# A written order for three engines, from the output projection to the FFN's activation sums of a decoder layer

## The chip, the cores and the metric

The kernel runs on one core of a Trainium2 chip. The metric is the device time of one execution in microseconds (us); lower is better. Engines: TensorE (PE) multiplies matrices and transposes, VectorE (DVE), ScalarE (ACT) and GpSimd (POOL) work elementwise, SyncE (SP) issues the DMAs. Each engine runs its own queue in order; semaphores make one wait for another.

## The reference

One decoder layer on a sequence of 1024 tokens of width 1024, in float32. What matters here is the second half of the mixer and the start of the FFN (D_FF is 2816):

```python
m = jnp.concatenate([rmsnorm(a, attn_group_norm[i]),
                     rmsnorm(c, conv_group_norm[i])], axis=-1)
x = x + rmsnorm(m @ w_out[i], mix_post_norm[i])
h = rmsnorm(x, ffn_pre_norm[i])
f = (jax.nn.silu(h @ w_gate[i]) * (h @ w_up[i])) @ w_down[i]
```

Here `a` is the causal attention's output, `c` the gated convolution's; `rmsnorm` divides a row by its root mean square and multiplies by a gain.

## The kernel before

**Numbers.** Every float32 operand of a matmul is split into a high part (a cast to the type float32r, on ScalarE) and a low part (the operand minus the high part, on VectorE or GpSimd); `split` issues the cast and the subtraction one behind the other. A product is three matmuls: high by high, high by low, low by high.

**Memory.** `mr` and `mf` are arenas of 2 KB units in on-chip memory for split and for plain float32 data. They hand out the units that were freed longest ago within a named region; `ML` is the region of 22 units (eleven row tiles) in which rows of y, x and the raw copies live. `ps` hands out the eight banks of the accumulator memory in turn.

**Output projection.** Tokens are eight tiles of 128 rows (T = 8). The convolution's half of the projection has been done before and waits in memory as y. For tile t, `wo_a` multiplies the attention half (24 matmuls with 512 columns, into two banks), adds y on VectorE (L1071) and issues the mean square of the sum on ScalarE (L230); `rstd_of` makes the reciprocal root of it, an addition on VectorE (L226) and a power on GpSimd (L227). `wo_x1` applies the norm and its gain (L1077), adds the rows of x (L1079), stores x1 and issues the second mean square. `wo_n` applies the FFN's norm (L1086), in place. `h2_turn` transposes the tile with eight PE transposes (L1106) into two banks, one for each half of the width (q = 0, 1), and makes of them a plain copy (L1108, L1110) and a split for the FFN's right operands. The loop runs over T + 3 steps with the tiles staggered: step t does `wo_a(t)`, `wo_x1(t-1)`, `wo_n(t-2)` and `h2_turn(t-3)`.

**FFN.** The gate and up products are done in 2 by 2 blocks with seven products in place of eight. B11 and B21 are the two halves of the width for tokens 0 to 511, B12 and B22 for tokens 512 to 1023. Three products use blocks as they are (B11, B21, B22); four use the activation sums T3 = B22 - B12, T2 = T3 + B11, T1 = B22 - T2 and T4 = B21 - T2, each 2048 columns wide on VectorE, split by `t_split`. Raw B11 and B21 go through memory (`hr_d`). Weights come in pairs `fp` of two 128-column blocks for gate and up (m = 0, 1); `raw_load` fetches them, `factor` makes the left operand of product p (sums on VectorE for pair 0, on GpSimd otherwise) and splits it, `product` does twelve matmuls and takes the bank's result out. The products 1 and 2 of pairs 0, 1 and 2 need no activation sum and are done first; then a loop over all that is left follows, five factors ahead.

**Order.** The program is written as one stream, and a scheduler decides the order of each engine's queue from it by its own model of times.

Of the kernel before, what the change touches and what calls it, by code (L numbers as in the profile page):

```python
# [135 lines left out]
def hybrid_layer(ctx: ExitStack, tc: tile.TileContext, x, x_t, p_t, cols_in, positions,  # L136
# [924 lines left out]
    def row_norm(t, i):  # L1061
        r = ss_y[:, 2 * t + i : 2 * t + i + 1]
        junk = mr(2, BJ)
        mean_sq(junk.a, rows_y[t].a, D, r)
        free(junk)
        rstd_of(r)

    def wo_a(t):
# [2 lines left out]
        dve.scalar_tensor_tensor(y, b, ss_a[:, t : t + 1], y, op0=ALU.mult, op1=ALU.add)  # L1071
        ps.put(ids)
        row_norm(t, 0)

    def wo_x1(t):
# [5 lines left out]
        sp.dma_start(x1_d[t * P : (t + 1) * P, :], y)
        row_norm(t, 1)

    def wo_n(t):
        y = rows_y[t].a
        dve.scalar_tensor_tensor(y, y, ss_y[:, 2 * t + 1 : 2 * t + 2], g_ffn.a, op0=ALU.mult,  # L1086
                                 op1=ALU.mult)

# [7 lines left out]
    def h2_turn(t):  # L1096
        src = rows_y.pop(t)
# [4 lines left out]
        for q in range(2):  # L1102
            ids, b = ps.get()
            for j in range(4):
                k = 4 * q + j
                pe.transpose(b[:, j * P : (j + 1) * P], src.a[:, k * P : (k + 1) * P], ident[:])  # L1106
# [146 lines left out]
    head = [(0, m, p) for p in (1, 2) for m in range(2)]  # L1253
    for t in range(T + 3):
        if t < T:
            wo_a(t)
        elif t == T:
            for d in (mTa, wo):
                for h, l in d.values():
                    free(h, l)  # L1260
            for i in head[:2]:
                product(*i)
        elif t == T + 1:
            for i in head[2:]:
                product(*i)
# [352 lines left out]
```

## Time and profile before

| | |
|---|---|
| median of 3 runs | 1230.39 us (1228.6, 1230.39, 1286.19) |
| the profiled execution | 1227.49 us |
| its span, first to last instruction | 1225.4 us |
| mean granted TensorE clock | 0.990 |
| busy in the span: PE, DVE, ACT, POOL | 1201.5, 810.6, 587.3, 503.8 us |

The profile shows one execution. A row of the timeline has the start, the duration, the engine, the line in the code, the operation with output and input, and in brackets the idle time before it and what ended it. Where a row shows x2, two instructions that follow each other were merged. A row of the stages has the stretch, its length, each engine's busy time, the granted clock as a share of full speed, the DMA engines' busy share and GB/s.

### The profile page before, as it was taken

How to read it: one execution, taken by the hardware profiler on the slowest of the kernel's cores; microseconds unless marked ns; L12 is line 12 of the kernel's file. 1: busy time of each engine (PE TensorE's matmuls, PEld its weight loads, DVE VectorE, ACT ScalarE, POOL GpSimd, SP SyncE). 2: the span in 40 equal slices, each digit the busy share in tenths (PEclk: the TensorE clock that was granted, in tenths of full speed). 3: DMA queues.
4: the chain of work that ended last, by engine and by line, in shares of the span. 5: the costliest groups of instructions: out<-in, count | busy, mean ns of one | idle time of the engine just before them, and what ended most of it. 6: DMA issues, size and time to landing. Idle time of an engine off the chain costs nothing.

```text
span 1225.4 us, 16706 instructions
## 1 busy us (share of the span) xinstructions
PE 1201.5 (98%) x5918; PEld 1012.2 (83%) x5918; DVE 810.6 (66%) x1173; ACT 587.3 (48%) x1079; POOL 503.8 (41%) x392
## 2 busy tenths in 40 slices
PE   8999999999999999789999999999999999999998
PEld 6998888889999888678788888888888888888886
DVE  6676346478867758785657665565556677758775
ACT  7543333267766736543433333333345546545652
POOL 4433534226554311025888646674634102202321
PEclk8999999999999999889999999999999999999999
DMA  8712553994561667524465445543566576654342
GB/s 267 258 39 104 184 202 133 278 365 90 135 161 44 232 223 252 203 104 143 161 229 197 140 144 190 178 157 118 209 209 200 184 242 230 233 172 164 120 136 79
DMA packets 89821, 217.77 MB, mean 178 GB/s; under 512 B 9030, under 2 KB 18026, under 8 KB 88426
## 3 DMA queue, kind: packets, MB, share of 16 engines
q1 hardware_dynamic: 89392, 216.17, 53.4%
q8 instruction: 46, 0.75, 0.3%
q10 hardware_dynamic: 346, 0.54, 0.2%
q14 instruction: 37, 0.30, 0.1%
HBM read 145.38 MB, written 71.04 MB: 177 GB/s over the span
## 4 chain that ended last, share of the span: by engine, by line
PE 80%; DVE 6%; DMA 5%; issue 3%; ACT 3%; POOL 2%; ACTq 0%; POOLq 0%; DVEq 0%; SPq 0%
PE banks L1192 10%; PE banks L1195 10%; PE banks L1194 10%; PE banks L220 7%; PE banks L222 7%; PE banks L221 7%; PE banks L1391 6%; PE banks L1390 6%; PE banks L1389 6%; PE banks L894 2%; DVE mem_r L210 2%; PE banks L1498 1%; PE banks L1501 1%; PE banks L1500 1%; PE banks L865 1%
## 5 line engine op out<-in xcount | busy, mean ns | idle before, releaser
L210 DVE TENSOR_TENSOR mem_r<-mem_f,mem_r 128x512 fp32r<-128x512 f32 (+1 forms) x404 | 374.4, 958 | 206.4 <-ACT mem_r L209 194.1
L209 ACT CAST mem_r<-mem_f 128x512 fp32r<-128x512 f32 (+2 forms) x407 | 258.4, 666 | 410.6 <-PE banks L1194 128.7
L1192 PE MATMUL banks<-mem_r 128*128 128x512 f32 x616 | 242.0, 393 | 4.5 <-ACT mem_r L209 3.4
L1194 PE MATMUL banks<-mem_r 128*128 128x512 f32 x616 | 241.6, 392 | 0.0
L1195 PE MATMUL banks<-mem_r 128*128 128x512 f32 x616 | 240.8, 392 | 0.1
L220 PE MATMUL banks<-mem_r 128*128 128x512 f32 (+2 forms) x536 | 196.3, 371 | 2.4 <-ACT mem_r L209 1.7
L221 PE MATMUL banks<-mem_r 128*128 128x512 f32 (+2 forms) x536 | 196.4, 368 | 1.3 <-POOL mem_r L210 1.2
L222 PE MATMUL banks<-mem_r 128*128 128x512 f32 (+2 forms) x536 | 196.0, 368 | 0.0
L1192 PEld LDWEIGHTS banks<-mem_r 128*128 128x128 f32 x616 | 116.5, 189 | 30.7 <-ACT mem_r L209 5.0
L1195 PEld LDWEIGHTS banks<-mem_r 128*128 128x128 f32 x616 | 116.7, 189 | 25.7 <-DVE mem_r L210 1.1
L1194 PEld LDWEIGHTS banks<-mem_r 128*128 128x128 f32 x616 | 116.8, 190 | 24.3 <-DVE mem_r L210 0.2
L1391 PE MATMUL banks<-mem_r 128*128 128x512 f32 x308 | 119.8, 389 | 0.0
L1390 PE MATMUL banks<-mem_r 128*128 128x512 f32 x308 | 119.8, 389 | 0.0
L1389 PE MATMUL banks<-mem_r 128*128 128x512 f32 x308 | 119.8, 390 | 0.0
L220 PEld LDWEIGHTS banks<-mem_r 128*128 128x128 f32 x536 | 101.2, 190 | 19.1 <-ACT mem_r L209 2.8
L221 PEld LDWEIGHTS banks<-mem_r 128*128 128x128 f32 x536 | 101.6, 190 | 17.4 <-POOL mem_r L210 1.4
L222 PEld LDWEIGHTS banks<-mem_r 128*128 128x128 f32 x536 | 101.5, 189 | 16.1
L879 POOL TENSOR_TENSOR mem_f<-mem_f,stats 128x640 f32<-128x640 f32 (+5 forms) x64 | 73.4, 1161 | 92.0 <-DVE stats L878 49.4
L227 POOL TENSOR_TENSOR small<-small,mhalf 128x1 f32<-128x1 f32 (+2 forms) x46 | 37.6, 821 | 177.5 <-DVE small L226 177.0
L1210 DVE TENSOR_TENSOR mem_f<-banks,mem_f 128x512 f32<-128x512 f32 x66 | 45.2, 686 | 55.9 <-PE banks L1195 55.8
L210 DVE TENSOR_TENSOR mem_r<-banks,mem_r 128x512 fp32r<-128x512 f32 (+3 forms) x118 | 69.3, 612 | 12.9 <-ACT mem_r L209 12.3
L1390 PEld LDWEIGHTS banks<-mem_r 128*128 128x128 f32 x308 | 57.8, 188 | 12.0
(197 smaller groups left out, 1890.0 us busy)
## 6 DMA issues: line engine op xcount, KB each, us to landing
sc_d<-mem_f SPq DMA_DIRECT2D x77, 256.0 KB, 3.5
mem_f<-sc_d SPq DMA_DIRECT2D x77, 256.0 KB, 3.0
mem_f<-in_w_gate_dram SPq DMA_DIRECT2D x22, 512.0 KB, 5.2
mem_f<-in_w_up_dram SPq DMA_DIRECT2D x22, 512.0 KB, 5.1
mem_f<-in_w_down_dram SPq DMA_DIRECT2D x22, 512.0 KB, 4.5
wc_d<-mem_f SPq DMA_DIRECT2D x22, 512.0 KB, 2.7
mem_f<-wc_d SPq DMA_DIRECT2D x44, 256.0 KB, 3.1
mem_f<-in_w_down_dram SPq DMA_DIRECT2D x33, 256.0 KB, 3.4
```

What stands on the lines that cost most here:

```text
L209: act.copy(h, src)
L210: (eng or dve).tensor_tensor(l, src, h.bitcast(F32), op=ALU.subtract)
L220: pe.matmul(o, wh, vh, start=i == 0, stop=False)
L221: pe.matmul(o, wh, vl, start=False, stop=False)
L222: pe.matmul(o, wl, vh, start=False, stop=i == n - 1)
L879: pool.tensor_tensor(pt.a[:, 0:n], pt.a[:, 0:n], sm.to_broadcast([P, n]), op=ALU.mult)
L1192: pe.matmul(b, wh.a[:, c], th[:, k], start=first and k == 0, stop=False, skip_group_check=True)
L1194: pe.matmul(b, wh.a[:, c], tl[:, k], start=False, stop=False, skip_group_check=True)
L1195: pe.matmul(b, wl.a[:, c], th[:, k], start=False, stop=k == 3, skip_group_check=True)
L1389: pe.matmul(b, ah.a[:, c], bh.a, start=first, stop=False, skip_group_check=True)
L1390: pe.matmul(b, ah.a[:, c], bl.a, start=False, stop=False, skip_group_check=True)
L1391: pe.matmul(b, al.a[:, c], bh.a, start=False, stop=last, skip_group_check=True)
```

## The change

The stretch from the loop to the last activation sum is put under a manual schedule for PE, DVE and ACT: these three queues take the instructions of the stretch in the order in which the code writes them (later instructions may still be put between them); POOL and SP are scheduled as before. For this the helpers are cut in pieces. `row_norm` becomes `row_sq` and `row_rstd`; `h2_turn` becomes `turn_pe` (transposes), `turn_cast`, `turn_copy`, `turn_dve` (subtractions) and `turn_put`; `factor` becomes `factor_a` (sums and cast) and `factor_d` (subtraction); `product` becomes `product_mm` and `product_end`; `t_split` becomes `t_cast` and `t_low`. `wo_n` writes the norm into the rows that held x, not in place. T2, and later T4, are made in B12's buffer instead of one of their own. Pair 2's first half is loaded into the row region `ML`. y of a tile is loaded one step ahead instead of two.

```diff
     def wo_x1(t):
...
-        free(xr)
+        rows_n[t] = xr
         sp.dma_start(x1_d[t * P : (t + 1) * P, :], y)
-        row_norm(t, 1)
+        row_sq(t, 1)
     def wo_n(t):
-        y = rows_y[t].a
-        dve.scalar_tensor_tensor(y, y, ss_y[:, 2 * t + 1 : 2 * t + 2], g_ffn.a, op0=ALU.mult,
+        y = rows_y.pop(t)
+        dve.scalar_tensor_tensor(rows_n[t].a, y.a, ss_y[:, 2 * t + 1 : 2 * t + 2], g_ffn.a, op0=ALU.mult,
                                  op1=ALU.mult)
+        free(y)
...
+    def turn_cast(t):
+        for q, b, h, l in turn_places(t):
+            act.copy(h, bank3(b, 4))
+
+    def turn_copy(t):
...
+        for q, (ids, b) in enumerate(turned[t]):
             if first:
                 act.copy(raw.a[:, q * U : (q + 1) * U], b)
             else:
                 act.copy(four(tr[q])[:, :, o], bank3(b, 4))
...
+    def turn_dve(t, only):
+        for q, b, h, l in turn_places(t):
+            if q == only:
+                dve.tensor_tensor(l, bank3(b, 4), h.bitcast(F32), op=ALU.subtract)
...
+    def wo_step(t, fill=()):
         if t < T:
+            wo_mm(t)
+        for i in fill:
+            factor_a(*i)
+        if t >= 3:
+            turn_cast(t - 3)
+        if 1 <= t <= T:
+            wo_a(t - 1)
+        if t >= 3:
+            turn_copy(t - 3)
+        if 2 <= t <= T + 1:
+            row_rstd(t - 2, 1)
+        for i in fill:
+            factor_d(*i)
+        if t >= 3:
+            turn_dve(t - 3, 0 if t - 3 < T // 2 else 1)
+        if 2 <= t <= T + 1:
+            wo_n(t - 2)
+        if 1 <= t <= T:
+            row_rstd(t - 1, 0)
+        if t >= 3:
+            if t - 3 < T // 2:
+                turn_dve(t - 3, 1)
+            turn_put(t - 3)
+        if 2 <= t <= T + 1:
+            turn_pe(t - 2)
         if 1 <= t <= T:
             wo_x1(t - 1)
         if t < T:
             load_x(t)
...
+        if 1 <= t < T - 1:
+            load_y(t + 1)
+    EN = mybir.EngineType
+    with tc.manual_schedule(engines={EN.PE, EN.DVE, EN.Activation}):
+        for t in range(T):
+            wo_step(t, {1: ((0, 0, 1), (0, 1, 1)), 2: ((0, 0, 2), (0, 1, 2))}.get(t, ()))
...
+        both(product_mm, 0, 1)
+        wo_step(T)
...
+        both(product_mm, 0, 2)
+        wo_step(T + 1)
...
+        raw_load(2, 0, ((0, 22),))
...
+        both(factor_a, 1, 1)
+        product_end(0, 0, 2)
+        factor_d(1, 0, 1)
+        product_mm(1, 0, 1)
...
+        t_sum(b12.a, b22.a, b12.a, ALU.subtract)
+        both(product_mm, 1, 2)
+        t_cast("T3", b12.a)
+        both(product_end, 1, 1)
+        factor_a(0, 0, 6)
+        t_low("T3", b12.a)
+        factor_d(0, 0, 6)
+        factor_a(2, 0, 1)
+        t_sum(b12.a, b12.a, b11, ALU.add)
+        factor_d(2, 0, 1)
+        product_end(1, 0, 2)
+        product_mm(2, 0, 1)
...
+        t_sum(b12.a, b21, b12.a, ALU.subtract)
+        both(factor_a, 0, 5)
+        both(factor_d, 0, 5)
```

VectorE's queue within the loop, before, about a step and a half of it (L226 the addition of `rstd_of`, L1077 and L1079 `wo_x1`, L210 from banks the subtraction of `h2_turn`, L1071 `wo_a`, L1086 `wo_n`):

```order
L226 TENSOR_SCALAR small<-small 128x1
L1077 SCALAR_TENSOR_TENSOR mem_f<-mem_f,small 128x1024
L226 TENSOR_SCALAR small<-small 128x1
L1079 TENSOR_TENSOR mem_f<-mem_f 128x1024
L210 TENSOR_TENSOR mem_r<-banks,mem_r 128x4x128
L1071 SCALAR_TENSOR_TENSOR mem_f<-banks,small,mem_f 128x1024
L210 TENSOR_TENSOR mem_r<-banks,mem_r 128x4x128
L1086 SCALAR_TENSOR_TENSOR mem_f<-mem_f,small 128x1024
```

VectorE's queue for one step now (L1077 `wo_a`, L1145 `turn_dve`, L1094 `wo_n`, L1083 and L1085 `wo_x1`); every step from the third to the sixth reads so:

```order
L1077 SCALAR_TENSOR_TENSOR mem_f<-banks,small,mem_f 128x1024
L226 TENSOR_SCALAR small<-small 128x1
L1145 TENSOR_TENSOR mem_r<-banks,mem_r 128x4x128
L1094 SCALAR_TENSOR_TENSOR mem_f<-mem_f,small 128x1024
L226 TENSOR_SCALAR small<-small 128x1
L1145 TENSOR_TENSOR mem_r<-banks,mem_r 128x4x128
L1083 SCALAR_TENSOR_TENSOR mem_f<-mem_f,small 128x1024
L1085 TENSOR_TENSOR mem_f<-mem_f 128x1024
```

The tile's norm `wo_n` now stands in each step between the two subtractions of the tile ahead of it, and `wo_x1` of the next tile behind both.

ScalarE's queue at the first transposed tile, before (L230 the mean squares, L1108 the copy of a bank, L209 its cast):

```order
L230 ACTIVATE mem_r,small<-mem_f 128x1024 x7
L1108 COPY mem_f<-banks 128x512
L209 CAST mem_r<-banks 128x4x128
L1108 COPY mem_f<-banks 128x512
L209 CAST mem_r<-banks 128x4x128
L230 ACTIVATE mem_r,small<-mem_f 128x1024
```

And now (L1219 the cast of `factor_a`, L1126 of `turn_cast`, L1135 the copy of `turn_copy`):

```order
L230 ACTIVATE mem_r,small<-mem_f 128x1024 x2
L1219 CAST mem_r<-mem_f 128x512 x2
L230 ACTIVATE mem_r,small<-mem_f 128x1024 x2
L1126 CAST mem_r<-banks 128x4x128 x2
L230 ACTIVATE mem_r,small<-mem_f 128x1024
L1135 COPY mem_f<-banks 128x512 x2
```

Before, copy and cast of a bank followed each other; now both casts come first, then the mean square of `wo_a`, then both copies.

VectorE's queue around the first activation sums, before (L1303 a sum, L210 2048 wide the subtraction of `t_split`, L210 512 wide that of `factor`):

```order
L1303 TENSOR_TENSOR mem_f<-mem_f 128x2048
L210 TENSOR_TENSOR mem_r<-banks,mem_r 128x4x128
L1303 TENSOR_TENSOR mem_f<-mem_f,mem_r 128x2048
L210 TENSOR_TENSOR mem_r<-mem_f,mem_r 128x2048
L210 TENSOR_TENSOR mem_r<-mem_f,mem_r 128x512
L1303 TENSOR_TENSOR mem_f<-mem_f 128x2048
```

And now (L1308 a sum, L1317 `t_low`, L1189 `factor_d`, L1205, L1206 and L1214 sums of pair 0's factors, L1260 the addition of `product_end`):

```order
L1308 TENSOR_TENSOR mem_f<-mem_f 128x2048
L1205 TENSOR_TENSOR mem_f<-mem_f 128x512
L1206 TENSOR_TENSOR mem_f<-mem_f 128x512
L1214 TENSOR_TENSOR mem_f<-mem_f 128x512
L1317 TENSOR_TENSOR mem_r<-mem_f,mem_r 128x2048
L1189 TENSOR_TENSOR mem_r<-mem_f,mem_r 128x512
L1308 TENSOR_TENSOR mem_f<-mem_f,mem_r 128x2048
L1189 TENSOR_TENSOR mem_r<-mem_f,mem_r 128x512
L1260 TENSOR_TENSOR mem_f<-banks,mem_f 128x512
```

Sums of pair 0's factors now stand between the first activation sum and its subtraction, and the subtraction for pair 2's first factor, the last L1189, behind T2's sum.

More of the change, by code (lines that the diff above doesn't have):

```diff
@@ L1094, in four, with turn_pe, turn_places @@
         return b.a.rearrange("p (k c) -> p k c", k=4)
-    def h2_turn(t):
-        src = rows_y.pop(t)
+    turned = {}
+    def turn_pe(t):
+        src = rows_n.pop(t)
+        turned[t] = [ps.get(), ps.get()]
+        for q, (ids, b) in enumerate(turned[t]):
+            for j in range(4):
+                k = 4 * q + j
+                pe.transpose(b[:, j * P : (j + 1) * P], src.a[:, k * P : (k + 1) * P], ident[:])
+        free(src)
+    def turn_places(t):
+        o = slice(t % 4 * P, (t % 4 + 1) * P)
+        for q, (ids, b) in enumerate(turned[t]):
+            if t < T // 2 or q:
+                h, l = tf["B" + "12"[q] + "12"[t >= T // 2]]
+                yield q, b, four(h)[:, :, o], four(l)[:, :, o]
+    def turn_cast(t):
+        for q, b, h, l in turn_places(t):
+            act.copy(h, bank3(b, 4))
+    def turn_copy(t):
         o = slice(t % 4 * P, (t % 4 + 1) * P)
@@ L1101, in h2_turn @@
             raw = mf(2, ML)
[L1102 to L1106, printed above, removed]
+        for q, (ids, b) in enumerate(turned[t]):
             if first:
@@ L1188, in product @@
         th, tl = (four(v) for v in tf[RIGHT[p]])
-        first, last = p in (1, 2, 5), p in (2, 3, 4)
+        first = p in (1, 2, 5)
         for k in range(4):
@@ L1252, in hybrid_layer, with both, t_sum, t_cast @@
     tr[0], tr[1] = mf(4, ((22, 26),)), mf(4, ((26, 30),))
-    head = [(0, m, p) for p in (1, 2) for m in range(2)]
-    for t in range(T + 3):
-        if t < T:
[L1256 to L1265, printed above, removed]
+    def both(f, fp, p):
+        for m in range(2):
+            f(fp, m, p)
+    def t_sum(o, x, y, op):
+        dve.tensor_tensor(o, x, y, op=op)
+    def t_cast(n, v):
+        if n not in tf:
+            tf[n] = pair(4, BT)
+        act.copy(tf[n][0].a, v)
+    def t_low(n, v):
+        h, l = tf[n]
+        dve.tensor_tensor(l.a, v, h.a.bitcast(F32), op=ALU.subtract)
+    def wo_step(t, fill=()):
+        if t < T:
+            wo_mm(t)
[23 more added lines that the diff above has]
+            turn_pe(t - 2)
         if 1 <= t <= T:
@@ L1281, in hybrid_layer @@
-        if t + 2 < T:
-            load_y(t + 2)
-        if t == T - 1:
-            raw_load(0, 1, ML)
-        if t == T:
-            raw_load(1, 0, ML)
-        if t == T // 2:
-            for i in head:
-                factor(*i)
-    b12, b22 = tr[0], tr[1]
-    def both(f, fp, p):
-        for m in range(2):
-            f(fp, m, p)
-    def t_split(n, v):
-        if n not in tf:
-            tf[n] = pair(4, BT)
-        h, l = tf[n]
-        split(h.a, l.a, v)
-    def t_sum(o, x, y, op):
-        dve.tensor_tensor(o, x, y, op=op)
```

124 lines of the change are left out of this document (75 added, 49 removed).

## The prediction

> **What bounds the kernel now.** I read the shares and the slices on the page first, then the stages, then each wait of TensorE.
>
> ```profile
> PE 1201.5 (98%) x5918; PEld 1012.2 (83%) x5918; DVE 810.6 (66%) x1173; ACT 587.3 (48%) x1079; POOL 503.8 (41%) x392
> ...
> PE   8999999999999999789999999999999999999998
> ```
>
> TensorE is busy for 98% of the span, and only slices 16 and 17 (490 to 551 us) dip inside it. So a change can only win what TensorE loses there, and it loses whenever it makes TensorE wait. The stages say the same.
>
> ```profile
> 430.00:485.00 55.00, 55.00 (x264) 45.75 (x263) 38.34 (x50) 26.23 (x49) 9.77 (x13) 1.00 0.72 231
> 485.00:605.00 120.00, 108.14 (x460) 86.82 (x459) 90.69 (x95) 54.12 (x88) 49.82 (x36) 0.93 0.44 152
> 605.00:700.00 95.00, 95.00 (x421) 78.67 (x420) 62.48 (x63) 34.02 (x60) 71.60 (x49) 1.00 0.54 189
> ```
>
> The columns are length, then busy time of PE, PEld, DVE, ACT and POOL, then the granted clock. The output projection's loop (to 485) runs without a gap at full clock; the 120 us behind it lose 11.9 us and some clock; from 605 TensorE is full again. The timeline of TensorE names the losses:
>
> ```profile
> 505.09 1.94 PE L1106 MATMUL banks<-ident,mem_f 128*128 128x128 f32 x8 [7.34 <-issue]
> 507.37 0.79 PE L1192 MATMUL banks<-mem_r 128*128 128x512 f32 x1 [0.34 <-ACT mem_r L209]
> 525.31 0.79 PE L1192 MATMUL banks<-mem_r 128*128 128x512 f32 x1 [3.09 <-ACT mem_r L209]
> ...
> 497.80:505.10 7.30, 0.01 (x1) 0.04 (x1) 2.81 (x6) 1.15 (x2) 0.00 (x0) 0.68 1.00 369
> 505.10:510.90 5.80, 5.46 (x17) 4.30 (x18) 5.49 (x8) 3.73 (x7) 0.93 (x1) 0.52 0.63 253
> 522.20:525.30 3.10, 0.02 (x1) 0.00 (x0) 3.10 (x4) 0.66 (x2) 0.00 (x0) 0.85 0.47 163
> 525.30:531.40 6.10, 6.09 (x15) 4.79 (x16) 6.10 (x6) 3.28 (x4) 0.00 (x0) 0.52 0.01 3
> ```
>
> Idle: 7.34 + 0.34 + 3.09 = 10.8 us. After both long gaps the granted clock is 0.52 for 5.80 and 6.10 us, which costs 0.48 x 11.9 = 5.7 us more. Two further gaps of about 0.5 us, at 583 and 592, lie behind the region and I leave them in. **At most 16.5 us can be won.**
>
> What ends the two long gaps:
>
> ```profile
> 497.95 0.33 SPq L1081 DMA_DIRECT2D x_d<-mem_f  x1
> 503.71 1.28 DVE L1086 SCALAR_TENSOR_TENSOR mem_f<-mem_f,small 128x1024 f32<-128x1024 f32 x1 [4.39 <-DMA x_d<-mem_f]
> ...
> 518.87 2.88 DVE L210 TENSOR_TENSOR mem_r<-mem_f,mem_r 128x2048 fp32r<-128x2048 f32 x2
> 521.18 0.33 SPq L1148 DMA_DIRECT2D mem_f<-in_w_up_dram  x1
> 524.64 2.42 ACT L209 CAST mem_r<-mem_f 128x512 fp32r<-128x512 f32 x2 [3.21 <-DMA mem_f<-in_w_up_dram]
> ```
>
> The last tile's second norm (L1086) overwrites the rows that the store of x1 is still reading, and the transposes wait for it. The load of w_up for pair 2 goes into the buffer of B12, so it is issued only when the subtraction of T3 (the 2048-wide L210) has read it.
>
> **The change, part by part.** *What it removes.* The norm now writes into the rows of x, so no store stands before it: the 7.34 goes. Pair 2 is loaded into the row region, not into B12: the 3.09 goes. The 0.34 and both stretches of slow clock go with them: minus 16.5 us. TensorE's own work stays: 64 transposes and as many matmuls as before.
>
> *What it adds: a chain in every step of the loop.* TensorE needs for a step 24 matmuls and 8 transposes.
>
> ```profile
> 466.79 0.39 PE L222 MATMUL banks<-mem_r 128*128 128x512 f32 x1
> ...
> 474.05 0.39 PE L221 MATMUL banks<-mem_r 128*128 128x512 f32 x1
> 474.28 1.03 PE L1106 MATMUL banks<-ident,mem_f 128*128 128x128 f32 x8
> 475.07 0.48 PE L222 MATMUL banks<-mem_r 128*128 128x512 f32 x1
> ```
>
> Between the first two rows lie 32 starts in 7.26 us, 0.227 each; the transposes take 0.79. A step is 24 x 0.227 + 0.79 = 6.24 us. VectorE must now follow ScalarE through each step in the written order. Durations of the links, from start to next start:
>
> ```profile
> 446.24 0.15 DVE L226 TENSOR_SCALAR small<-small 128x1 f32<-128x1 f32 x1 [1.22 <-ACT mem_r L230]
> 446.48 0.55 POOL L227 TENSOR_TENSOR small<-small,mhalf 128x1 f32<-128x1 f32 x1 [3.05 <-DVE small L226]
> 447.06 1.28 DVE L1077 SCALAR_TENSOR_TENSOR mem_f<-mem_f,small 128x1024 f32<-128x1024 f32 x1 [0.66 <-POOL small L227]
> ...
> 458.62 1.28 DVE L1077 SCALAR_TENSOR_TENSOR mem_f<-mem_f,small 128x1024 f32<-128x1024 f32 x1
> 459.81 1.28 DVE L1071 SCALAR_TENSOR_TENSOR mem_f<-banks,small,mem_f 128x1024 f32<-128x1024 f32 x1
> 461.01 1.22 DVE L1079 TENSOR_TENSOR mem_f<-mem_f 128x1024 f32<-128x1024 f32 x1
> ...
> 462.32 1.06 ACT L230 ACTIVATE mem_r<-mem_f 128x1024 fp32r<-128x1024 f32 x1
> 463.28 0.19 ACT L230 ACTIVATION_READ_ACCUMULATOR mem_r<-mem_f 128x1 f32 x1
> 463.38 0.57 ACT L1108 COPY mem_f<-banks 128x512 f32<-128x512 f32 x1
> 463.84 0.59 ACT L209 CAST mem_r<-banks 128x512 fp32r<-128x512 f32 x1
> 464.32 0.60 ACT L1108 COPY mem_f<-banks 128x512 f32<-128x512 f32 x1
> ...
> 482.17 1.28 DVE L210 TENSOR_TENSOR mem_r<-banks,mem_r 128x512 fp32r<-128x512 f32 x2
> 483.37 1.28 DVE L1086 SCALAR_TENSOR_TENSOR mem_f<-mem_f,small 128x1024 f32<-128x1024 f32 x1
> ```
>
> The built program lets turn_dve wait not for the cast of its bank, but for the *copy* out of the same bank, and wo_step writes that copy behind the next tile's square. So from the end of the residual sum (L1085): handover 0.04, square of x1 1.06, two casts 0.96, square of the next sum 1.06, copy 0.57, handover 0.04, first subtraction 0.60, the norm L1094 1.20, then from the rstd's addition to the end of the power 0.82 (the second subtraction hides in it), L1083 1.31 (its result is needed at once), L1085 1.22. Sum **8.9 us a step against 6.24**. Behind the waiting subtraction stand wo_n, wo_x1 and the next wo_a on VectorE; for wo_n waits turn_pe, and behind it TensorE's next projection. TensorE therefore idles 2.6 us in each step from the third. In the last two it does FFN products in place of projections, also 24 matmuls, so they pay the same. That is seven transposes, turn_pe(1) to turn_pe(7); the first pays about 2.0, since step 2 (no turn yet) leaves VectorE some tenths ahead: 2.0 + 6 x 2.6 = **17.6 us**. In steps 7 to 9 one cast less is made, but the subtraction waits for the second copy: the same length.
>
> *What it moves: the activation sums.* From turn_pe(7) to the first use of T1 (product 5 of pair 0) TensorE has 8 transposes, ten products of 12 matmuls and two matmuls more: 0.8 + 122 x 0.227 = 28.5 us. VectorE has in the same stretch, by the order as built, seven 2048-wide operations and 29 that are 512 wide.
>
> ```profile
> 504.97 0.68 DVE L1162 TENSOR_TENSOR mem_f<-mem_f 128x512 f32<-128x512 f32 x1
> 505.69 0.69 DVE L1163 TENSOR_TENSOR mem_f<-mem_f 128x512 f32<-128x512 f32 x1
> ...
> 513.86 2.29 DVE L1303 TENSOR_TENSOR mem_f<-mem_f 128x2048 f32<-128x2048 f32 x1 [0.77 <-ACT mem_f L1110]
> 516.07 0.68 DVE L210 TENSOR_TENSOR mem_r<-banks,mem_r 128x512 fp32r<-128x512 f32 x1
> ```
>
> 7 x 2.21 + 29 x 0.62 (0.60 apart, 0.72 where the next needs the result) = 33.5 us, and some 2.2 us of waits for ScalarE (a Silu with a cast in front of pair 2's second factor, the 1.9 us cast of T1). 35.7 - 28.5 = **7 us** of idle: about 2.9 before the first product of pair 2, whose subtraction stands behind T3's and the T2 sum, the rest before product 5. GpSimd does only the 16 powers there, so no slower VectorE is to be charged.
>
> *The clock.* The gap of 3.10 us above was granted 0.85 on average, so the clock fell about 2.2 us into it; gaps of 2.6 may do it too. While VectorE sets the pace, a slow stretch only fills the next gap and costs nothing. Behind the last gap (about 3.8) nothing covers it: 0.48 x 6.0 = **2.9 us**.
>
> *Nothing for the rest.* The split of casts and subtractions adds no instruction. The loads of y, x and the weights stay behind their stores on SP, but land ahead of use as I count it: y of a tile is issued a step and a half before wo_a, and 512 KB took 3 to 5 us. The nearest is pair 1's second half, behind the store of x1(6) on SP with perhaps 1 us in hand; late, it would cost 0 to 3 us, and I take 0. Bounds: the loop's link lengths can err by 0.25 a step (1.8 in all), the sums by 2, the clock by 0 to 6.
>
> *Sum*, against the profiled execution of 1227.5: 1227.5 - 16.5 + 17.6 + 7.0 + 2.9 = 1238.5. The median shown lies 2.9 above that execution, the lowest run 1.1 above; I forecast **1239 us**, 0.7% above the median. A measurement of this kernel tells about 2% from no change, so that reads as no change.
>
> **The rivals.** *1, the gaps close.* VectorE's own issue time in a step is only 4 x 1.2 + 2 x 0.6 + 0.1 = 6.1 us, below 6.24; if ScalarE's work did not stand between, the loop would be free and the early loads would help: down to 1227.5 - 16.5 = 1211, with half of the activation sums' gaps 1215. Against it: ScalarE, at 48% over the span, is not full, but its squares and copies stand in line between VectorE's own operations, and the waits count them. The Trainium skill ("PSUM — Partial Sum Buffer", section "PSUM bank collisions raise a hardware error") has two engines that read one bank at the same time collide, reads included, so that they have to be ordered; that fits a wait on the copy, which no row of before shows apart from the cast (there the copy comes first). *2, only the copy does not count*: the chain loses the second square and the copy, 1.6 us, so a step is 7.3; the loop then costs 7 x 1.1 = 7.5, but the later stages, no longer held back, catch up with VectorE and their loads and idle some 4 more: 1227.5 - 16.5 + 7.5 + 11 + 2.9 = 1232. *3, slower:* the clock falls in the first gap and stays at 0.52 to the end of the loop, because TensorE never has a full stretch of work. Then a step is 12.5 us, not 8.9: 7 x 3.6 = 25 more, 1264. It decides from the point where slow work longer than 8.9 us a step makes TensorE the pace. Against it: twice the clock came back after 5.8 to 6.1 us of work, and slow work leaves no gap. The Trainium skill ("TensorE: Matmul & The Clock Gate", Part 1) lets the clock fall only after an idle window of about 3.4 us, by which gaps of 2.6 would cost nothing and this rival would get no chance; the row of the 3.10 us gap, in which it fell after some 2.2, differs, and the row keeps 0.04 for it. *4, the written order doesn't hold*, the scheduler keeps its own: then 1227 to 1230; the order as built speaks against it.
>
> **How the numbers follow.** Forecast 0.78, rival 1 0.09, rival 2 0.07, rival 3 0.04, rival 4 0.02. The forecast's own range is 1232 to 1247 (links, sums, clock, run to run). To leave out no more than 2 in 10 with doubts on rival 2, I give 1228 to 1248. Faster by over 2% would be below 1206, which not even all 16.5 us reach: 0.01. Slower by over 2% is above 1255: rival 3 and a little of the forecast's tail: 0.05. Within 2%: 0.94.
>
> **What would show it.** Right: from the third step of the loop TensorE idles 2 to 3 us at each group of transposes, released by L1094; VectorE idles some 2.3 us at L1145, released by ScalarE's L1135 or L1137; starts of L1077 lie 8.9 us apart; no wait on the store of x1, none for w_up; gaps of about 3 and 4 us before pair 2's first product and product 5. Wrong: the loop without gaps, L1145 released by L1126, steps of 6.3 us, or a granted clock near 0.5 through the loop.

## The result, and the profile after

| | median us | lowest to highest | ratio to before, 95% interval |
|---|---|---|---|
| before, in the runs beside it | 1228.6 | 1227.31 to 1286.19 | |
| after | 1237.71 | 1236.27 to 1239.22 | 1.0077 [1.006, 1.0094] |

Ratios, here and below, leave out executions far above the others of their kernel: this one at 1286 us and one of e8 at 1704.71 us, which is the one that e8's trace shows. The changed kernel is 0.8% slower, clear of its interval, but less than the 2% that the prediction took as what can be told from no change; the forecast was 1239. Its profiled execution took 1239.22 us, the highest of its five, with a span of 1237.0 against 1225.4 before. First the page, TensorE's share and its 40 slices:

```profile
PE 1203.3 (97%) x5918; PEld 1014.2 (82%) x5918; DVE 818.9 (66%) x1173; ACT 586.3 (47%) x1079; POOL 505.4 (41%) x392
...
PE   8999999999999998879999999999999999999998
```

TensorE is as busy as before; the dip begins in slice 15 (464 us), not in slice 16, and is three slices wide. Then the stages (length, busy time of PE, PEld, DVE, ACT and POOL, granted clock, DMA share, GB/s), for the loop from its second group of transposes, the first that waits, to its last, for the stretch from the end of the first gap behind it to the end of the second, and for the 6 us behind that:

```profile
460.90:514.10 53.20, 42.38 (x192) 34.24 (x193) 36.12 (x46) 25.23 (x48) 6.48 (x12) 0.94 0.74 256
...
529.00:551.50 22.50, 18.71 (x75) 14.97 (x75) 19.10 (x21) 11.26 (x16) 0.00 (x0) 0.91 0.06 24
551.50:557.50 6.00, 6.00 (x14) 4.74 (x15) 4.81 (x6) 4.04 (x5) 1.36 (x1) 0.50 0.27 87
```

The first row is six steps in 53.2 us, **8.87 us a step**. TensorE has 192 instructions there, six steps of 32, which need 6 x 6.24 = 37.4 us: 15.8 us are lost. The rows of TensorE's timeline say where (start, duration, line, and in brackets the idle time before it and what ended it; six of the rows with a gap):

```profile
460.90 1.09 PE L1113 MATMUL banks<-ident,mem_f 128*128 128x128 f32 x8 [1.86 <-DVE small L226]
...
478.68 1.48 PE L1113 MATMUL banks<-ident,mem_f 128*128 128x128 f32 x8 [2.35 <-DVE small L226]
...
487.52 1.07 PE L1113 MATMUL banks<-ident,mem_f 128*128 128x128 f32 x8 [0.70 <-DVE small L226]
...
514.11 1.06 PE L1113 MATMUL banks<-ident,mem_f 128*128 128x128 f32 x8 [2.30 <-DVE mem_f L1094]
...
529.02 0.50 PE L1241 MATMUL banks<-mem_r 128*128 128x512 f32 x1 [2.49 <-DVE mem_r L1189]
...
551.49 0.79 PE L1241 MATMUL banks<-mem_r 128*128 128x512 f32 x1 [3.77 <-DVE mem_r L1189]
```

Each group of transposes (L1113) waits for the norm L1094; the name L226 beside it is the tiny addition that follows that norm on VectorE. Where the idle time is only 0.70, the step before was run in part at a low clock, and the slow work filled the gap. One step of VectorE and of ScalarE shows why the norm is late:

```profile
464.02 1.28 DVE L1077 SCALAR_TENSOR_TENSOR mem_f<-banks,small,mem_f 128x1024 f32<-128x1024 f32 x1
...
467.81 0.69 DVE L1145 TENSOR_TENSOR mem_r<-banks,mem_r 128x512 fp32r<-128x512 f32 x1 [2.33 <-ACT mem_f L1135]
468.41 1.28 DVE L1094 SCALAR_TENSOR_TENSOR mem_f<-mem_f,small 128x1024 f32<-128x1024 f32 x1
...
472.87 1.28 DVE L1077 SCALAR_TENSOR_TENSOR mem_f<-banks,small,mem_f 128x1024 f32<-128x1024 f32 x1
...
464.14 1.06 ACT L230 ACTIVATE mem_r<-mem_f 128x1024 fp32r<-128x1024 f32 x1 [4.73 <-DVE mem_f L1085]
...
465.20 1.05 ACT L1126 CAST mem_r<-banks 128x512 fp32r<-128x512 f32 x2
...
466.14 1.07 ACT L230 ACTIVATE mem_r<-mem_f 128x1024 fp32r<-128x1024 f32 x1
...
467.19 1.07 ACT L1135 COPY mem_f<-banks 128x512 f32<-128x512 f32 x2
```

The casts end at 466.2. The subtraction L1145 starts at 467.81, when the first of the two copies merged in the row of 467.19 has ended. Between cast and copy stands a square (L230). So VectorE is idle for 2.33 us in every step.

The last stage, whose code the diff does not touch, is longer too. Its first product (with the weights `w_ple_gate`) is at 1137.96 before and 1146.07 after, its end at 1225.4 and 1237.0: 87.4 against 90.9 us.

### The profile page after: what moved, and what is told of

Read it like the earlier page. It is cut to its first block, busy times and chain, and to the rows that moved or that the text cites. A ratio compares the mean times of both kernels' runs of the same rounds, so it can differ in the third digit from the quotient of the medians.

```text
span 1237.0 us, 16688 instructions
## 1 busy us (share of the span) xinstructions
PE 1203.3 (97%) x5918; PEld 1014.2 (82%) x5918; DVE 818.9 (66%) x1173; ACT 586.3 (47%) x1079; POOL 505.4 (41%) x392
## 4 chain that ended last, share of the span: by engine, by line
PE 85%; DVE 6%; ACT 3%; DMA 3%; issue 2%; POOL 1%; SPq 0%; ACTq 0%; DVEq 0%; POOLq 0%
PE banks L1241 11%; PE banks L1238 11%; PE banks L1240 11%; PE banks L220 7%; PE banks L222 7%; PE banks L221 7%; PE banks L1489 6%; PE banks L1490 6%; PE banks L1488 6%; PE banks L894 2%; PE banks L1600 1%; PE banks L1597 1%; PE banks L1599 1%; PE banks L865 1%; PE banks L922 1%
## 5 line engine op out<-in xcount | busy, mean ns | idle before, releaser
L210 DVE TENSOR_TENSOR mem_r<-mem_f,mem_r 128x512 fp32r<-128x512 f32 (+1 forms) x246 | 202.6, 863 | 115.6 <-ACT mem_r L209 111.5
L209 ACT CAST mem_r<-mem_f 128x512 fp32r<-128x512 f32 (+2 forms) x249 | 157.5, 674 | 195.2 <-PE banks L1489 71.7
L1189 DVE TENSOR_TENSOR mem_r<-mem_f,mem_r 128x512 fp32r<-128x512 f32 x154 | 170.1, 1118 | 78.8 <-ACT mem_r L1219 78.1
L1219 ACT CAST mem_r<-mem_f 128x512 fp32r<-128x512 f32 x154 | 93.7, 621 | 202.9 <-PE banks L1240 119.8
L1241 PEld LDWEIGHTS banks<-mem_r 128*128 128x128 f32 x616 | 116.9, 190 | 31.6 <-DVE mem_r L1189 7.1
L1240 PEld LDWEIGHTS banks<-mem_r 128*128 128x128 f32 x616 | 116.9, 190 | 24.5
L1238 PEld LDWEIGHTS banks<-mem_r 128*128 128x128 f32 x616 | 117.0, 190 | 24.2
L220 PEld LDWEIGHTS banks<-mem_r 128*128 128x128 f32 x536 | 101.2, 190 | 18.8 <-ACT mem_r L209 2.2
L221 PEld LDWEIGHTS banks<-mem_r 128*128 128x128 f32 x536 | 101.7, 190 | 17.5 <-POOL mem_r L210 1.4
L222 PEld LDWEIGHTS banks<-mem_r 128*128 128x128 f32 x536 | 101.5, 189 | 16.3
L227 POOL TENSOR_TENSOR small<-small,mhalf 128x1 f32<-128x1 f32 (+2 forms) x46 | 37.9, 826 | 168.3 <-DVE small L226 167.7
L1260 DVE TENSOR_TENSOR mem_f<-banks,mem_f 128x512 f32<-128x512 f32 x66 | 45.2, 685 | 51.6 <-PE banks L1241 51.6
```

Of the source, the lines that this page charges most:

```text
L209: act.copy(h, src)
L210: (eng or dve).tensor_tensor(l, src, h.bitcast(F32), op=ALU.subtract)
L220: pe.matmul(o, wh, vh, start=i == 0, stop=False)
L221: pe.matmul(o, wh, vl, start=False, stop=False)
L222: pe.matmul(o, wl, vh, start=False, stop=i == n - 1)
L1189: dve.tensor_tensor(l.a, src, h.a.bitcast(F32), op=ALU.subtract)
```

## The experiments

All are compared with the kernel before, run beside them on the same chip (its median is 1226.2 to 1226.8 us there). Ratios, for overview:

| run | what it is | median us | ratio, 95% interval |
|---|---|---|---|
| e1 | after, copy ahead of the square | 1233.76 | 1.0064 [1.0052, 1.0076] |
| e2 | after, copy behind the subtractions | 1235.15 | 1.0082 [1.0068, 1.0095] |
| e3 | after, casts and copies behind their transposes | 1229.41 | 1.0028 [1.0016, 1.0041] |
| e4 | before, with the two removals alone, last tile | 1223.64 | 0.9982 [0.9971, 0.9993] |
| e5 | before, with the two removals alone, last two tiles | 1222.72 | 0.9975 [0.9963, 0.9987] |
| e6 | after, block sums on GpSimd | 1242.79 | 1.0135 [1.0112, 1.0158] |
| e7 | e3, weight loads changed over | 1224.2 | 0.9989 [0.9975, 1.0002] |
| e8 | e7 with the sums of e6 | 1234.29 | 1.0062 [1.0041, 1.0084] |
| e9 | after, norm back in its own rows | 1239.01 | 1.0101 [1.0088, 1.0115] |
| e10 | e6, GpSimd in the written order | 1241.07 | 1.012 [1.0103, 1.0137] |
| e11 | e8, GpSimd in the written order | 1229.78 | 1.0032 [1.0018, 1.0046] |
| e12 | e7, pair 2's factors first | 1230.72 | 1.0031 [1.0017, 1.0046] |

### What sets the step of the loop: e1, e2, e3

e1:

```diff
         if t >= 3:
             turn_cast(t - 3)
+            turn_copy(t - 3)
         if 1 <= t <= T:
             wo_a(t - 1)
-        if t >= 3:
-            turn_copy(t - 3)
```

> The changed kernel with one move on ScalarE: turn_copy(t-3) stands right behind turn_cast(t-3), ahead of the square that wo_a(t-1) issues. Theory A (the subtraction L1145 waits for the copy out of its bank, and the copy stands behind that square): the chain of a step loses one square, 1.06 us, so steps of the loop go from 8.87 to about 7.8 us, the idle time ahead of L1145 from 2.33 to about 1.3, and the time falls by about 7 x 1.06, to 1229 to 1232. Rival B (VectorE's or ScalarE's total work, or the cast, sets the step): steps stay at 8.9 and the time at 1236 to 1238.

VectorE in e1, one step:

```profile
471.30 1.28 DVE L1077 SCALAR_TENSOR_TENSOR mem_f<-banks,small,mem_f 128x1024 f32<-128x1024 f32 x1
...
474.05 0.69 DVE L1145 TENSOR_TENSOR mem_r<-banks,mem_r 128x512 fp32r<-128x512 f32 x1 [1.29 <-ACT mem_f L1135]
...
479.11 1.28 DVE L1077 SCALAR_TENSOR_TENSOR mem_f<-banks,small,mem_f 128x1024 f32<-128x1024 f32 x1
```

The wait is 1.29 and the step 7.81 us, each one square shorter, as theory A has it. The stretch from the second to the last transposes of the loop takes 48.0 us, 5.2 less than in the changed kernel. Behind the loop a cast now waits 1.76 us for pair 1's w_up, and the gaps there are 7.6 us instead of 6.3. By the traces some 0.3% should be left as a gain; the ratio fell by 0.13%, and the intervals allow for 0.3%. The time, 1233.76, lies above theory A's range.

e2:

```diff
-        if t >= 3:
-            turn_copy(t - 3)
         if 2 <= t <= T + 1:
             row_rstd(t - 2, 1)
...
                 turn_dve(t - 3, 1)
+            turn_copy(t - 3)
             turn_put(t - 3)
```

> The changed kernel with turn_copy(t-3) written behind the tile's last subtraction, ahead of turn_put(t-3). Theory A (the order of reads of one bank is what the subtraction waits for): now L1145 waits only for the cast of its bank: .04 + 1.06 (square of x1) + .48 + .04, then .60 + 1.20 + .82 + 1.31 + 1.22, a step of about 6.8; the idle time ahead of L1145 goes from 2.33 to about 0.3 and is released by L1126; the time falls to 1223 to 1227. Rival B: the copies now wait for VectorE and delay the next square of x1 on ScalarE; then steps stay over 8 us and the time over 1233.

VectorE and ScalarE in e2:

```profile
476.10 1.28 DVE L1077 SCALAR_TENSOR_TENSOR mem_f<-banks,small,mem_f 128x1024 f32<-128x1024 f32 x1
...
478.14 0.69 DVE L1145 TENSOR_TENSOR mem_r<-banks,mem_r 128x512 fp32r<-128x512 f32 x1 [0.33 <-ACT mem_r L1126]
...
483.20 1.28 DVE L1077 SCALAR_TENSOR_TENSOR mem_f<-banks,small,mem_f 128x1024 f32<-128x1024 f32 x1
...
484.00 0.59 ACT L1135 COPY mem_f<-banks 128x512 f32<-128x512 f32 x1 [4.36 <-DMA hr_d<-mem_f]
```

With the copy last, the subtraction waits 0.33 us for the cast of its bank (L1126), so it was the order of the two reads of one bank, not the cast. The Trainium skill ("PSUM — Partial Sum Buffer", section "PSUM bank collisions raise a hardware error") lists ScalarE's and VectorE's reads of one bank among the pairs that must be ordered; e1 and e2 agree in that VectorE's read waits for those of ScalarE's reads of its bank that are written ahead of it, and no others. Steps are 6.83 and 7.10 us, then 8.49: the copy now waits for the store hr_d out of the buffer that it fills. And the loop's end came early for the loads: TensorE waits 3.57 us for pair 1's first cast, which waits 4.68 us for its w_gate, then 2.96 us for pair 2's first cast, and the last stage has a gap of 2.52. So the time did not fall at all; theory A was right on the wait and wrong on the total.

e3:

```diff
-        if t >= 3:
-            turn_cast(t - 3)
...
-        if t >= 3:
-            turn_copy(t - 3)
...
             turn_pe(t - 2)
+            if t <= T:
+                turn_cast(t - 2)
+                turn_copy(t - 2)
         if 1 <= t <= T:
             wo_x1(t - 1)
```

> The changed kernel with turn_cast and turn_copy of a tile written right behind its transposes, a step earlier, ahead of the square of x1. Theory A (the pace is the chain through ScalarE): casts and copies lie beside the residual sum, L1145 finds them done and does not wait; the chain of a step is the next sum 1.24, the subtraction 0.6, the norm 1.2, the rstd 0.82, L1083 1.31, L1085 1.22 and some tenths, 6.4 to 6.7 us against TensorE's 6.24; the loop's gaps fall from 12.7 to 3 us or less, the time to 1221 to 1226. Rival B (VectorE's own work is the pace): steps of 8 us or more, 1233 or more.

VectorE in e3, one step, then ScalarE and TensorE behind the loop:

```profile
475.28 1.28 DVE L1077 SCALAR_TENSOR_TENSOR mem_f<-banks,small,mem_f 128x1024 f32<-128x1024 f32 x1
...
476.71 0.68 DVE L1145 TENSOR_TENSOR mem_r<-banks,mem_r 128x512 fp32r<-128x512 f32 x1
...
481.91 1.28 DVE L1077 SCALAR_TENSOR_TENSOR mem_f<-banks,small,mem_f 128x1024 f32<-128x1024 f32 x1
...
503.83 0.62 ACT L1219 CAST mem_r<-mem_f 128x512 fp32r<-128x512 f32 x1 [6.37 <-DMA mem_f<-in_w_gate_dram]
...
504.50 0.80 PE L1238 MATMUL banks<-mem_r 128*128 128x512 f32 x1 [4.66 <-ACT mem_r L1219]
```

L1145 has no wait, the step is 6.63 us, and of the loop's 12.7 us of gaps 0.5 are left. That settles the cause of the loop's cost. Part of the gain was lost again behind the loop: pair 1's w_gate, asked for at 496 us, lets its cast start only at 503.83, and gaps of 4.66, 3.11, 2.99 and 0.84 follow, 11.6 us where the changed kernel has 6.3. The kernel is 0.5% faster than the changed one, still 0.3% slower than before, and above theory A's 1221 to 1226.

### What the removals alone are worth: e4, e5, e9

e4 is the kernel before with the norm of tile 7 in other rows, and pair 2's load in the row region (T2 is then summed in place):

```diff
-        y = rows_y[t].a
-        dve.scalar_tensor_tensor(y, y, ss_y[:, 2 * t + 1 : 2 * t + 2], g_ffn.a, op0=ALU.mult,
+        y = rows_y[t]
+        if t == T - 1:
+            rows_y[t] = last[0]
+        dve.scalar_tensor_tensor(rows_y[t].a, y.a, ss_y[:, 2 * t + 1 : 2 * t + 2], g_ffn.a, op0=ALU.mult,
...
-    raw_load(2, 0)
+    raw_load(2, 0, ((0, 22),))
```

> The kernel before with the two removals alone: the last tile's norm writes into other rows, and pair 2's weights are loaded into the row region; no written order. Theory A (the sum's first term): both gaps and their slow clock go, 16.5 us, 1210 to 1214. Rival B (only the wait for the store, 4.39 us of the 7.34, goes, since the norm L1086 would otherwise have started at 499.3 and TensorE is out of work from 497.8): a gap of about 3 us stays there and the clock falls in it: 1215 to 1219. Rival C (the scheduler arranges the rest anew and a new wait takes their place): 1222 or more.

TensorE and VectorE in e4:

```profile
507.19 1.94 PE L1112 MATMUL banks<-ident,mem_f 128*128 128x128 f32 x8 [7.89 <-issue]
...
505.80 1.28 DVE L1090 SCALAR_TENSOR_TENSOR mem_f<-mem_f,small 128x1024 f32<-128x1024 f32 x1 [4.75 <-DMA x_d<-mem_f]
...
508.18 1.28 DVE L1090 SCALAR_TENSOR_TENSOR mem_f<-mem_f,small 128x1024 f32<-128x1024 f32 x1 [0.44 <-POOL small L227]
```

Two norms follow each other, and the first one waits: it is tile 6's, so the prediction had the wrong tile ("the last tile's second norm"), and e4 mended the wrong one. The load's gap fell from 3.09 to 0.99. e5 adds tile 6 (its norm goes into the rows of its x, and the first products are written behind it):

```diff
-        free(xr)
+        if t == T - 2:
+            last[t] = xr
+        else:
+            free(xr)
...
```

> Like the run before it (the kernel before with the removals alone), but with the norms of the last two tiles in other rows: the trace of that run shows the norm that waits for a store of x1 to be the seventh tile's, not the eighth's. Theory A (the store is what ends the 7 us gap, and the rest of it, some 2.9 us, is VectorE's lag behind TensorE): no wait on a store of x1, that gap 2 to 3.5 us, no gap over 1 us behind it, 1216 to 1220. Rival B (the whole 7.34 goes and the slow clock with it, as the sum had it): 1210 to 1214. Rival C (a load or a store that lands late takes its place): a new gap released by a DMA, 1222 or more.

TensorE and ScalarE in e5, and a wait of the DMA queue between 493 and 504 us (total, times, longest):

```profile
507.29 0.80 PE L1199 MATMUL banks<-mem_r 128*128 128x512 f32 x1 [7.42 <-ACT mem_r L209]
...
503.06 1.14 ACT L209 CAST mem_r<-mem_f 128x512 fp32r<-128x512 f32 x2 [7.23 <-DMA mem_f<-in_w_up_dram]
...
SPq L1155 <- DMA x_d<-mem_f: 6.4, 1, 6.4
```

No norm waits for a store, and a gap of 7.42 us stands in the same place, released by a cast that waits for weights: rival C. The store had hidden a load that was as late. And the store is not out of the chain: the next load, of w_gate, stands 6.4 us in the DMA queue until the store of x1 has landed, and its cast comes just ahead of the gap's end. The DMA engines are busy for 1.00 of that gap in the kernel before (the prediction's row from 497.80) and for 0.92 of it in e5, so perhaps transfers as such are late there; no run made them fewer. With all that the two edits take away, the kernel before gains 0.25%, some 3 us, not 16.5. Some of the difference was lost in the last stage: the profiled execution reaches it 5.7 us sooner than that of before, and is 4.2 us longer in it. e5 is the fastest version of the study by its median; with e4 it is faster than both kernels by more than its interval, though by far less than the 2%.

e9 undoes that part in the changed kernel:

```diff
-        rows_n[t] = xr
+        free(xr)
...
-        y = rows_y.pop(t)
-        dve.scalar_tensor_tensor(rows_n[t].a, y.a, ss_y[:, 2 * t + 1 : 2 * t + 2], g_ffn.a, op0=ALU.mult,
+        y = rows_n[t] = rows_y.pop(t)
+        dve.scalar_tensor_tensor(y.a, y.a, ss_y[:, 2 * t + 1 : 2 * t + 2], g_ffn.a, op0=ALU.mult,
...
-        free(y)
```

> The changed kernel with one part undone: the second norm writes back into the rows that the store of x1 is still reading. Theory A (in the written order the norm stands some 7 us behind the sum that the store reads, and the store takes about 5, so the other rows hide nothing that the order doesn't hide already): no gap of TensorE over 3 us from a store, 1236 to 1240, level with the changed kernel. Rival B (the sum's first term: the other rows are what takes the 7 us away): the wait for a store is back at the last two tiles, with slow clock behind it, 1243 to 1248.

VectorE's waits in e9 (total, times, longest):

```profile
DVE mem_f L1094 <- DMA x_d<-mem_f: 2.7, 2, 1.7
```

The wait for a store is back with 2.7 us in all, and the ratio goes from 1.0077 to 1.0101, some 3 us (the intervals leave nothing to 6). That is nearer to theory A, though one gap of TensorE, 4.15 us at 498.86, is longer than it allowed: inside the written order the other rows are worth some 3 us, not 7, since the norm comes so late there that the store has mostly landed.

### The activation sums: e6, e10

e6:

```diff
-        eng = pool if fp else dve
+        eng = pool
...
-        t_sum(b12.a, b21, b12.a, ALU.subtract)
         both(factor_a, 0, 5)
         both(factor_d, 0, 5)
+        t_sum(b12.a, b21, b12.a, ALU.subtract)
```

> The changed kernel with less of VectorE's work ahead of product 5: pair 0's six block sums go to GpSimd, which does little but powers there, and the sum for T4 is written behind the factors of product 5. Theory A (the gaps of 2.49 and 3.77 us are VectorE's work of the region against TensorE's): VectorE has 4.3 + 2.2 us less ahead of product 5, both gaps together fall from 6.3 to 1.5 us or less, the slow clock behind them goes, the loop stays at 8.9 us a step, and the time falls by 5 to 9 us, to 1227 to 1231. Rival B (casts on ScalarE or loads end those gaps): they stay over 4 us, 1233 or more. Rival C (a sum of 512 takes GpSimd 1.5 us; six of them come too late for product 6): a gap before product 6 instead.

TensorE, GpSimd and VectorE in e6:

```profile
509.35 1.94 PE L1113 MATMUL banks<-ident,mem_f 128*128 128x128 f32 x8 [6.12 <-DVE small L226]
...
499.12 1.29 POOL L1214 TENSOR_TENSOR mem_f<-mem_f 128x512 f32<-128x512 f32 x1
500.37 0.55 POOL L227 TENSOR_TENSOR small<-small,mhalf 128x1 f32<-128x1 f32 x1
...
500.95 1.28 DVE L1083 SCALAR_TENSOR_TENSOR mem_f<-mem_f,small 128x1024 f32<-128x1024 f32 x1 [4.34 <-POOL small L227]
```

A step's power (L227) stood behind three block sums on GpSimd; the loop's chain runs through that power. So the run got slower for a reason that none of its three expectations named. Half of theory A came true: the gap before product 5 is gone, while 2.47 us stay before pair 2's first product. e10 puts GpSimd in the written order too:

```diff
-    with tc.manual_schedule(engines={EN.PE, EN.DVE, EN.Activation}):
+    with tc.manual_schedule(engines={EN.PE, EN.DVE, EN.Activation, EN.Pool}):
```

> Like the run with pair 0's six block sums on GpSimd, but with GpSimd in the written order too, so that these sums stand behind the last power. Theory A (there, 1242.8 us came from two powers that stood behind three sums each on GpSimd, 4.34 and 1.60 us of waiting at L1083, while the gap before product 5 fell as expected): L1083 waits under 1 us, no gap of 6 us, gaps before pair 2's first product and product 5 together under 3.5 us, 1229 to 1233. Rival B (GpSimd's sums slow VectorE's 512-wide subtractions beside them, which rose from 0.6 to 1.2 to 1.8 us in that trace wherever GpSimd was busy): gaps in the region stay at 6 us or more, 1236 or more.

VectorE and GpSimd in e10, ahead of pair 2's first product:

```profile
514.67 2.86 DVE L1189 TENSOR_TENSOR mem_r<-mem_f,mem_r 128x512 fp32r<-128x512 f32 x2
517.46 0.68 DVE L1260 TENSOR_TENSOR mem_f<-banks,mem_f 128x512 f32<-128x512 f32 x1
...
519.16 1.77 DVE L1189 TENSOR_TENSOR mem_r<-mem_f,mem_r 128x512 fp32r<-128x512 f32 x1
...
521.46 0.68 DVE L1189 TENSOR_TENSOR mem_r<-mem_f,mem_r 128x512 fp32r<-128x512 f32 x1
...
518.76 1.62 POOL L1214 TENSOR_TENSOR mem_f<-mem_f 128x512 f32<-128x512 f32 x1
```

The power's waits are those of the changed kernel again (2.6 us in all), the gap of 6.12 is gone, and so is the one before product 5. Yet the time is no better than e6's: gaps of 1.78 and 3.00 stand before pair 2's first product, for 2.49 in the changed kernel, and 0.86 and 2.71 later. Rival B is part of it. Until GpSimd's last sum ends at 520.4, three subtractions with both inputs in SBUF (L1189) take 1.43, 1.43 and 1.77 us; the next one, beside an idle GpSimd, takes 0.68. L1260, with one input in PSUM, takes 0.68 beside the sums too. The Trainium skill ("SBUF — State Buffer", section "Who interferes with whom") has a VectorE instruction with two SBUF inputs contend with a GpSimd instruction that reads SBUF, and one with fewer not; the rows agree. The three cost 2.6 us here, about what the gaps before pair 2 grew by; the later gap of 2.71 was not traced to its cause.

### In search of a faster one: e7, e8, e11, e12

e7 is e3 with the two loads at the loop's end exchanged (the two reads of `hr_d` are also written further back, but the traces have them issued at the same times, 487.7 and 488.1 us):

```diff
-        raw_load(0, 1, ML)
+        raw_load(1, 0, ML)
         both(product_mm, 0, 1)
         wo_step(T)
-        raw_load(1, 0, ML)
+        raw_load(0, 1, ML)
...
```

> The kernel with casts and copies behind their transposes, and the two weight loads at the loop's end changed over: pair 1's first half is asked for ahead of pair 0's second half. Theory A (the gaps of 4.66 and 3.11 us there are pair 1's weights, asked for at 496 and 505 us, too late for a loop that ends earlier): both gaps fall below 1.5 us, VectorE's work then shows as gaps of some 3 and 4 us before pair 2's first product and product 5, and the time falls by 3 to 6 us against that kernel (which was 3.1 us above the kernel before), so 3 us below to level with the kernel before. Rival B (pair 0's second half is now late, or VectorE's lag simply moves): no change, 3 us above.

TensorE in e7, its gaps behind the loop:

```profile
513.33 0.50 PE L1238 MATMUL banks<-mem_r 128*128 128x512 f32 x1 [2.35 <-ACT mem_r L1219]
...
517.06 0.80 PE L1241 MATMUL banks<-mem_r 128*128 128x512 f32 x1 [3.00 <-DVE mem_r L1189]
...
537.76 0.50 PE L1241 MATMUL banks<-mem_r 128*128 128x512 f32 x1 [0.84 <-DVE mem_r L1189]
```

The gap of 4.66 for pair 1's weights is gone, and the gaps are 5 us less in all. The gap of 3.11 is not gone: it stood before pair 2's first product, not pair 1's, so theory A had taken it for the wrong one, and here it is the 2.35. What is left, 6.2 us, is VectorE's work and what stands behind it in ScalarE's queue, and the kernel is level with before. e8 adds the edits of e6, e11 GpSimd in the written order besides:

> All three edits to the changed kernel: casts and copies behind their transposes, the weight loads changed over, and the sums off VectorE's path. Theory A (chain, loads and VectorE's work are all that the region loses): no gap over 1.5 us between 440 and 560 us, and 10 to 16 us below the kernel before: 1210 to 1217. Rival B (the last stage loses some us by its order as in the changed kernel, or a new wait arises in the region): 1218 to 1224.

> Casts and copies behind their transposes, weight loads changed over, T4's sum behind product 5's factors, and pair 0's block sums on GpSimd in the written order. Theory A: of the gaps of 2.35, 3.00 and 0.84 us in the kernel with casts and loads moved, 2 us or less are left in all, and the time falls 4 to 7 us below that kernel (which ran 2 us below the kernel before): 0.5% below before, 1217 to 1221. Rival B (GpSimd's sums slow VectorE beside them): level with that kernel or above, 1224 or more.

Both are slower than e7, by 0.7% and 0.4%: e8 lies above what either theory had, e11 where rival B put it. e8's trace is not read. In e11 the largest gaps are 3.40 and 3.78 us, before pair 2's first product. e12 takes e7 and writes another order behind the loop instead, with pair 2's factors ahead; the first of its edits is

```diff
         both(product_mm, 1, 2)
+        both(factor_a, 2, 1)
+        both(factor_d, 2, 1)
         t_cast("T3", b12.a)
...
```

> The kernel with casts and loads moved, and another written order behind the loop, with no work moved between engines: pair 2's factors stand ahead of T3's cast and subtraction and of the T2 sum, the T1 sum ahead of pair 2's second products' ends, T4's sum behind product 5's factors. Theory A (there the gaps of 2.35 and 3.00 us are pair 2's factor, which stands behind 2048-wide operations that it doesn't need): both gaps go, a gap of 2 to 4 us before product 6 and one of about 2 before product 5 remain, since VectorE's total stays; the time falls 3 to 5 us below that kernel, 0.3 to 0.6% below the kernel before. Rival B (VectorE's total sets the region whatever the order): the gaps move and keep their sum of 6 us; level with that kernel, 0 to 0.2% below before.

ScalarE and TensorE in e12:

```profile
511.79 0.62 ACT L1219 CAST mem_r<-mem_f 128x512 fp32r<-128x512 f32 x1 [5.93 <-DMA mem_f<-in_w_gate_dram]
...
591.49 0.50 PE L1238 MATMUL banks<-mem_r 128*128 128x512 f32 x1 [2.62 <-DVE mem_f L1260]
```

Neither theory: before pair 2's first product 1.36 us are left of 2.35 and 3.00, but its cast now waits 5.93 us for pair 2's w_gate, and all that is written behind it on ScalarE (T3's cast, the copies out of the banks) waits too; in e7 T3's cast ran in that time. Six more gaps of 0.2 to 2.6 us and one of 2.62 at 591 follow, and 5 us are lost against e7. A cast that is written ahead of its data holds up its whole queue.

## Why the prediction was right, point by point

**The wait on the copy: right.** L1145 is released by L1135 and L1137, idle 2.3 us, as forecast; e1 and e2 move the wait by moving nothing but the copy.

**The loop, 17.6 us: right to the tenth.** 1.86 at the first transposes that wait and 15.8 in the six steps. The step was forecast at 8.9 and measured 8.87. The forecast had all of it as gaps; in fact 12.7 us are gaps, and most of the rest is slow clock that fills some of them, which the part on the clock allowed for and priced at nothing.

**Minus 16.5: right as a loss of the kernel before, wrong as the worth of the edits.** Those two waits are absent from the changed trace. Counted by starts (each start to the next, less 0.227 us per matmul and 0.1 per transpose, over all of TensorE's rows from 425 us to the first down product) the kernel before loses 20.0 us there, since the two small gaps at 583 and 592, left in by the prediction, and what lies around each gap are in it. But e4, e5 and e9 show that the edits alone buy some 3 us in all, and e5's trace still loses 15.4 us there: behind the store stood a load, and it was tile 6's norm that waited. For this term the prediction never asked what is late next once the store's wait is gone. In the changed kernel the sum still comes out, since the whole stretch has another order there and its losses are in the terms that follow.

**The sums, 7.0, and the clock, 2.9: a little low.** Gaps of 2.49 and 3.77 us against 2.9 and some 4. From the last transposes of the loop to product 5 lie 37.4 us, against 35.7 forecast for VectorE; between the two gaps the clock is 0.91 on average. Behind the last gap 6.0 us at 0.50 cost 3.0, forecast 2.9. Counted by starts, the changed kernel loses 11.4 us there, for 9.9.

**Nothing for the rest: wrong by 3.5 us.** The last stage is untouched in the source, yet longer by 3.5. ScalarE and TensorE in it, after:

```profile
1167.28 0.59 ACT L1568 COPY mem_f<-banks 128x512 f32<-128x512 f32 x1 [4.60 <-DMA out_dram<-mem_f]
...
1175.73 0.79 PE L1600 MATMUL banks<-mem_r 128*128 128x512 f32 x1 [2.25 <-DVE mem_r L210]
```

A copy there waits 4.60 us for a store out of the buffer that it fills (1.06 and 1.38 in the kernel before); the block sums and subtractions behind it come late, and a gap of 2.25 with some slow clock follows. The scheduler had built another order of ScalarE and VectorE for this stage. All the rearranged kernels whose traces were read show that gap: 1.8 to 2.5 us in nine of them, with stages of 89.3 to 92.2 us, and 0.5 to 0.6 in e3 and e11, with 87.8 and 87.7, near the 87.4 of before. The wait itself does not tell them apart, for the copy waits 4.60 us in e3 too; but there it starts 19.5 us into the stage, 21.2 in the changed kernel, and the gap is shorter by nearly as much, 1.65. What makes the store land earlier there was not tried.

**The sum.** By starts, the region costs 28.8 for 20.0, 8.8 us more, where the forecast had 11.0. The last stage adds 3.5, the stages between 0.4, and the changed execution reached the region 1.1 us sooner, by 1.0 already at 188 us, ahead of all that was changed. Together 11.6 us of span (the medians differ by 9.1). So the forecast of 1238.5 against 1239.22 for the profiled execution owes some of its closeness to terms that cancel: that much is luck.

**The rivals.** 1 (gaps close) would have needed casts and copies out of the chain, which e3 does. 2 (only the copy doesn't count) is e2's wait, with a shorter step than the 7.3 forecast at first and then a new wait. 3 (slow clock throughout) is out: 0.94 in the loop. 4 is out: the written order held.

## What to carry to other kernels

When an order is written out by hand, two reads of one PSUM bank by two engines are a dependency in the order in which they are written: keep them next to each other, and place them where the waiting engine has other work (e3: 2.33 us of wait a step to none). A stall that ends in a named wait is worth only the distance to the next wait behind it; before it is priced, ask which load or store is late by nearly as much, and remove the wait in an experiment to see (e5: 7.42 us in the place of 7.34). Code that is not touched is still scheduled anew: price some us for it, either way, in a kernel where one order decides.
